# A hybrid attention and pooling layer: the first four blocks' order written out by hand, with scores between halves of projections

## The chip, the cores and the metric

The kernel runs on one core of one Trainium2 chip. Times are device microseconds of one execution. The program's engines are TensorE (PE, with its weight loads PEld), VectorE (DVE), ScalarE (ACT), GpSimd (POOL) and SyncE (SP), which issues all of the DMA transfers spoken of here.

## The reference

One layer of an encoder over 4096 tokens of width 1024: `x + RMSNorm_post(W_out [attn * silu(g_a) ; pool * silu(g_p)])`, where q, k, v, g_a, u_p and g_p come from one projection of the normed x.

```python
# q: 8 heads of 64; k, v: 2 heads; blocks of 128 queries see 3 blocks of keys
s = jnp.einsum('bnqkgd,bnskd->bnkgqs', qb, kw).astype(jnp.float32) * scale
s = jnp.where(valid, s + bias, NEG)               # |i - j| <= 128, T5 bias
m = jnp.maximum(jnp.max(s, axis=-1, keepdims=True), sk)   # learned sink
p = jnp.exp(s - m)
p = p / (jnp.sum(p, axis=-1, keepdims=True) + jnp.exp(sk - m))
o = jnp.einsum('bnkgqs,bnskd->bnqkgd', p, vw)
...
mean = (cg[:, hi] - cg[:, lo]) / (hi - lo)        # pooling windows 2, 4, 8, 16
y = (mean - u) @ pool_w[g] * pool_scale
```

## The kernel before

Every fp32 product is made of three fp16 products: each operand is kept as a high part and a rest, and PE multiplies high by high, high by rest and rest by high. So each result that PE needs again is read from its PSUM bank twice: ACT writes the high part and DVE (for Q, K and V, `split`, L1216 and L1217) or POOL (for the gated values, `low`, L1478) the rest. Until the second has been written, PE can neither use the result nor overwrite its bank.

The first stage, up to about 497 us, makes the projections g_p, u_p and g_a and leaves the pooling branch and the gates in DRAM (`yp_scr`, `ga_scr`). Its last part also makes K of unit 15. The second stage works on units of 256 tokens, from unit 15 down to 0. A unit u has the blocks 2u + 1 and 2u, of 128 queries each, and a block has two halves of four heads. Its steps on PE:

- `proj_k` and `proj_v` (L1361, L1365): K and V of the unit, 24 and 48 matmuls into one bank, kept by `keep_k` and `keep_v` (the tiles `k_all` and `vv`)
- `proj_q(u, half, bank)` (L1388): 48 matmuls, two pairs of heads of 24 each, into the bank `acc0` or `acc1` (tile `aq`), kept by `keep_q` (tile `q`)
- `scores(b, half)` (L1247, matmul L1272): 48 small matmuls into two banks of their own
- `values(b, bank)` (L1405, matmul L1422): probabilities by V, for both halves; one side goes to a bank of its own, the other to `acc0`, `acc1` or `acc2`
- `product` (L1564, matmul L1572): one of seven products of the gated values with pieces of W_out (`O11`, `O21`, `O22`, `OT1` to `OT4`, in the tiles `wo0` and so on, 1 MB each, loaded by `load_wo`, L1642), 12 matmuls of 512 columns. Seven products in place of eight come from sums of the halves (`sum1` to `sum4`, L1505 to L1516; the last on POOL).

Between scores and values lies the softmax of a half block: POOL copies the sink into the tile `p` (L1289), DVE makes logits and their maximum (L1295, four operations), ACT the exponentials (`exps`, L1306), DVE the denominators (L1313, L1316), ACT the scaled probabilities (`probs`, L1328), DVE their rests (`rests`, L1336), and SP issues a transposing DMA (`turn`, L1345, tile `pt`). The mixing of a unit goes on with `begin` (ACT copies one bank to the tile `mo0`, L1590), `gain11` (DVE, L1600), `add` (DVE, L1611), `square` (ACT, L1595), `gain` (POOL, L1606), `mean`, `residual` (DVE, L1633) and `store` (SP, L1639). The tiles `mo0` and `mo1` hold a block's result until its residual has been added.

The order of all of this is a plan: `due(t, fn, ...)` puts a step into a list with a time, and at the end (L1924) the list is sorted by these times and issued in that order, on every engine. The times are thus only an order; each engine works through its own queue and waits where an operand or a buffer is not ready. `pe(us, ...)` advances a clock `now[0]` for PE's steps, and `visit(b, half)` plans scores and softmax of a half block; `free` holds when DVE and ACT are through with the last one. Up to the second block from the end, one loop (L1743 to L1798) plans the steps of a block from these helpers; blocks 31 to 28 take branches of their own in it. The two last blocks are a table of numbers written by hand with `at_`, `soft` and `cast` (from L1802).

Of the kernel before, what the change touches and what calls it, by code (L numbers as in the profile page):

```python
# [17 lines left out]
P = 128  # L18
# [116 lines left out]
def hybrid_layer(ctx: ExitStack, tc, io, out):  # L135
# [74 lines left out]
    with ExitStack() as actx:  # L210
# [1032 lines left out]
    def due(t, fn, *args):  # L1243
        plan.append((t, len(plan), fn, args))
# [441 lines left out]
    def mix_p1(u):  # L1686
        due(pe(M, product, u, "11", O11, 0) - 1.0, begin, u)

    def mix_p4(u):
        pe(M, product, u, "22", OT4, 2)  # L1690

    def mix_p2(u):
        t = pe(M, product, u, "12", O21, 0, True)
        due(t, gain11, u)
        due(t + 0.1, square, u, 0, 0, 0)

    def mix_p6(u):
        due(pe(M, product, u, "s2", OT2, 1), add, u, (0, HI), (0, HI), 1)

    def mix_p7(u):  # L1700
        t = pe(M, product, u, "s3", OT3, 0)
        due(t - 2.0, add, u, (1, HI), (0, HI), 0)
        due(t - 1.9, add, u, (1, LO), (1, HI), 2)
        due(t + 1.4, square, u, 1, 0)
        due(t + 2.0, gain, u, 1, LO)

    def mix_p5(u):
        t = pe(M, product, u, "s1", OT1, 1)
        due(t, add, u, (1, HI), (1, HI), 1)
        due(t + 0.7, square, u, 1, 1)  # L1710
        due(t + 1.4, gain, u, 1, HI)
        finish(u, 1, t + 4.0)

    def mix_p3(u):
        t = pe(M, product, u, "s4", O22, 1, True)
        due(t, add, u, (0, HI), (0, HI), 1)
        due(t + 0.7, square, u, 0, 1)
        due(t + 1.4, gain, u, 0, HI)
        due(t + 4.0, mean, u, 0)
        due(t + 12.4, residual, u, 0, LO)  # L1720
        due(t + 13.1, residual, u, 0, HI)
        due(t + 13.8, store, u, 0, slice(0, D))

    def finish(u, i, t):

# [3 lines left out]

    u = NU - 1
    for o in (OT4, O11, O21, OT2):
        due(0.0, load_wo, o)
    due(0.1, load_gain)
    due(0.1, pool_in, u, 0)
    due(0.1, pool_in, u, 1)
    do_kv(u)

    due(now[0] + 1.0, lambda: nc.scalar.activation(dummy, mhalf, AF.Exp))  # L1740
    do_q(u, 0)
    now[0] += 1.0
    for b in reversed(range(2, NB)):  # L1743
        u = b // 2
        t0 = now[0]
        due(t0 + 10.0, load_ga, b)
        if b % 2 == 0 and 0 < b < NB - 2:
            due(t0 + 9.0, load_xr, u + 1, 1)
            due(t0 + 9.0, load_xr, u + 1, 0)
        visit(b, 0)  # L1750
        if b == NB - 1:
            do_q(u, 1, 2.8, 0)
            due(now[0] + 0.1, load_x, u - 2)
            now[0] += 2.5
            visit(b, 1)
            do_kv(u - 1, 2, 2.5)
            now[0] += 3.0
        elif b == NB - 3:
            due(free[1], load_wo, OT3)
            mix_p4(u + 1)  # L1760
            mix_p1(u + 1)
            attend(b + 1, 1)
            visit(b, 1)
            due(free[1], load_wo, OT1)
            due(free[1] + 8.0, load_wo, O22)
            do_kv(u - 1, 1)
            mix_p2(u + 1)
            mix_p6(u + 1)
        elif b % 2:
            mix_p3(u + 2)  # L1770
            do_kv(u - 1)
            attend(b + 1, 0)
            visit(b, 1)
            mix_p4(u + 1)
            mix_p1(u + 1)
            mix_p6(u + 1)
            mix_p2(u + 1)
        else:
            do_q(u - 1, 0, 2.0 * (b == NB - 2))
            if b < NB - 2:  # L1780
                attend(b + 1, 0)
            visit(b, 1)
            do_q(u - 1, 1, 2.0 * (b == NB - 2), int(b < NB - 2))
            due(now[0] + 2.1, load_x, u - 3)
            if b == NB - 2:
                attend(b + 1, 1)
            elif b > 2:
                mix_p7(u + 1)
# [11 lines left out]
    z = now[0]  # L1802
# [199 lines left out]
```

## Time and profile before

| | |
|---|---|
| median of 3 runs | 1193.59 us (1192.48 to 1194.16) |
| the profiled execution | 1192.04 us |
| its span in the trace | 1190.3 us |
| PE, DVE, ACT, POOL busy, share of the span | 97%, 79%, 59%, 25% |
| mean granted clock of PE | 0.997 |
| second stage's first four blocks | 497.3 to 583.5 us |
| the loop over the blocks behind them, and the end | 583.5 to 1092.3 us, and to 1190.3 us |

The profile's engines are as above; an engine's idle time is put down to what released it, so that `[2.88 <-ACT q L1216]` reads: idle for 2.88 us, until ACT's write of a tile `q` in line 1216 came. Tiles are shown there without their numbers. Busy time of PE counts pipelined matmuls whose ends are modelled. The granted clock is the share of full speed that the TensorE was given.

### The profile page before, as it was taken

What the parts mean: (1) busy time and instruction counts of PE and PEld (TensorE: products, weight loads), DVE (VectorE), ACT (ScalarE), POOL (GpSimd) and SP (SyncE); (2) the same over time, 40 slices, a digit from 0 to 9 for tenths busy, and PEclk for the clock granted to TensorE, in tenths of its full rate; (3) what the DMA queues carried; (4) which work ended last, traced back from release to release, by engine and by line L of the source; (5) the groups of instructions that cost most, each with busy time, mean ns of one, the idle gap of its engine ahead of it and who ended that gap; (6) DMA issues with size and microseconds to landing.
All of it is one profiled execution on the core that took longest, in us unless ns stands there. A gap on an engine that the chain in (4) does not pass through costs nothing. (4 is left out here: it accounts for less than half of the span.)

```text
span 1190.3 us, 33985 instructions
## 1 busy us (share of the span) xinstructions
PE 1154.4 (97%) x14304; PEld 884.8 (74%) x14304; DVE 941.9 (79%) x1879; ACT 703.8 (59%) x1459; POOL 303.4 (25%) x309
## 2 busy tenths in 40 slices
PE   5999999999999999998999999999999999999997
PEld 4998888888988888876667667576666667757643
DVE  6889996867888973567877878877887787787796
ACT  5865555545755541265666576666667667666662
POOL 0002111101101110203334434433533443343231
PEclk9999999999999999999999999999999999999999
DMA  9544587577657573397966876787886678586694
GB/s 318 208 124 151 169 277 246 171 239 259 221 169 249 156 212 117 117 242 174 253 181 147 188 189 128 200 196 142 192 193 177 145 191 192 135 190 164 156 245 124
DMA packets 292441, 224.65 MB, mean 189 GB/s; under 512 B 210704, under 2 KB 251920, under 8 KB 287680
## 3 DMA queue, kind: packets, MB, share of 16 engines
q1 hardware_dynamic: 292288, 222.48, 69.7%
q8 instruction: 112, 1.84, 0.6%
q14 instruction: 41, 0.34, 0.1%
HBM read 113.37 MB, written 60.33 MB: 146 GB/s over the span
## 5 line engine op out<-in xcount | busy, mean ns | idle before, releaser
L634 PEld LDWEIGHTS <-wq 128*128 128x128 f16 x4104 | 401.3, 98 | 53.1 <-issue 2.8
L634 PE MATMUL y<-xt,wq 128*128 128x256 f16 x1512 | 204.1, 273 | 0.9 <-ACT cc L742 0.9
L1336 DVE SCALAR_TENSOR_TENSOR pn<-p,rd,pn 128x384 f16<-128x384 f32 (+1 forms) x256 | 155.6, 654 | 31.8 <-ACT pn L1328 31.8
L1227 PE MATMUL aq<-xb,xb 128*128 128x256 f16 x1024 | 174.8, 274 | 1.7 <-DVE q L1217 1.6
L1306 ACT ACTIVATE p<-p,nm 128x385 f32<-128x385 f32 (+1 forms) x256 | 152.8, 598 | 33.3 <-POOL p L1289 22.4
L1572 PE MATMUL ms<-wo,ys 128*128 128x512 f16 x720 | 163.1, 379 | 1.7 <-ACT pn L1328 0.9
L1295 DVE CUSTOM_DVE_ANT_0 p<-s,nt,nsink 128x384 f32<-128x384 f32 (+1 forms) x256 | 155.9, 666 | 1.3 <-PE s L1272 1.1
L1328 ACT ACTIVATE pn<-p,rd 128x384 f16<-128x384 f32 (+1 forms) x256 | 136.4, 598 | 13.4 <-ACT p L1306 8.5
L1227 PEld LDWEIGHTS <-xb 128*128 128x128 f16 x1280 | 125.7, 98 | 23.3 <-issue 6.6
L1227 PE MATMUL aq<-xb,xt 128*128 128x256 f16 x512 | 140.3, 274 | 0.0
L1572 PEld LDWEIGHTS <-ys 128*128 128x128 f16 x720 | 69.0, 98 | 83.9 <-issue 3.3
L304 POOL TENSOR_TENSOR yt<-yt,sg 128x512 f32<-128x512 f32 (+2 forms) x32 | 48.0, 1501 | 311.3 <-DVE yt L307 302.3
L1572 PE MATMUL m<-wo,y 128*128 128x512 f16 x540 | 121.7, 379 | 2.8 <-ACT mo L1590 1.7
L1572 PEld LDWEIGHTS <-y 128*128 128x128 f16 x540 | 51.4, 98 | 68.3 <-issue 8.2
L1606 POOL TENSOR_TENSOR mo<-mo,gpost 128x512 f32<-128x512 f32 x39 | 63.6, 1630 | 86.8 <-ACT jkb L1595 85.7
L634 PE MATMUL plain<-xb,wq 128*128 128x256 f16 x576 | 68.8, 275 | 3.2 <-ACT xb L446 1.8
L1227 PEld LDWEIGHTS <-xt 128*128 128x128 f16 x640 | 62.9, 98 | 10.1 <-issue 1.5
L634 PE MATMUL y<-xb,wq 128*128 128x256 f16 x504 | 68.8, 273 | 0.0
L634 PE MATMUL v<-xb,wq 128*128 128x256 f16 x504 | 68.6, 273 | 0.2 <-DVE cc L304 0.2
L1272 PE MATMUL s<-k_all,q 64*32 64x288 f16 (+7 forms) x3648 | 62.9, 266 | 5.9 <-ACT q L1216 3.6
L634 PE MATMUL v<-xt,wq 128*128 128x256 f16 x504 | 68.6, 273 | 0.0
L634 PE MATMUL x<-xb,wq 128*128 128x256 f16 x504 | 68.3, 273 | 0.0
(211 smaller groups left out, 1917.1 us busy)
## 6 DMA issues: line engine op xcount, KB each, us to landing
nt<-in_xT SPq DMA_DIRECT2D x28, 512.0 KB, 5.2
x_scr<-xb SPq DMA_DIRECT2D x14, 1024.0 KB, 7.1
xb<-x_scr SPq DMA_DIRECT2D x14, 1024.0 KB, 7.6
xr<-in_x SPq DMA_DIRECT2D x28, 512.0 KB, 4.6
out<-xr SPq DMA_DIRECT2D x28, 512.0 KB, 2.8
xn<-in_x SPq DMA_DIRECT2D x27, 512.0 KB, 4.3
ga_scr<-cc SPq DMA_DIRECT2D x64, 128.0 KB, 2.2
raw<-in_w_out SPq DMA_DIRECT2D x16, 512.0 KB, 6.3
```

Source lines behind the costliest of these rows:

```text
L304: eng.tensor_tensor(out=out, in0=in0, in1=in1, op=op)
L634: nc.tensor.matmul(b[:, s], wq[:, slot[q, op], wv, s, k, :], x[:, xv, k, :], start=(first and k + s + wv + xv == 0), stop=(last and k == H ...
L1227: nc.tensor.matmul(acc, w[:, j, k, :], x[:, kh, v, kt, :], start=(n == 0), stop=(n == 3 * KT - 1),)
L1272: nc.tensor.matmul(s_ps[qs, gg, c0:c1], q_t[u, half][a, qi, jj, tl + 32 * hq : tl + 32 * hq + 32], k_all[a, ki, kc + c0 - s0 : kc + c1 - s ...
L1295: nc.vector.tensor_tensor_reduce(out=p_t[b, half][:, hh, :nk], in0=s_t[jj][:, gg, :nk], in1=bias[:, h, lo : lo + nk], scale=negc[:, h : h ...
L1306: nc.scalar.activation(p[:, hh, : nk + 1], p[:, hh, : nk + 1], AF.Exp, bias=nm_t[b, half][:, hh : hh + 1], scale=-1.0, accum_out=den_t[b, ...
L1328: nc.scalar.activation(prob_view(b, half)[:, 0, i], p_t[b, half][:, i, :nk], AF.Copy, scale=rd_t[b, half][:, i : i + 1],)
L1336: nc.vector.scalar_tensor_tensor(out=pn4[:, 1, i], in0=p_t[b, half][:, i, :nk], scalar=rd_t[b, half][:, i : i + 1], in1=pn4[:, 0, i], op0= ...
L1572: nc.tensor.matmul(z_t[u, tag], y[:, k, yi, :], wo[o][:, wi, k, :], start=(n == 0 and acc is None), stop=(n == 3 * HK - 1), skip_group_che ...
L1606: eng.tensor_tensor(out=mo, in0=mo, in1=gpost[:, cs], op=ALU.mult)
```

## The change

The blocks 31, 30, 29 and 28 leave the loop, and a table of numbers takes their place; the loop now begins at block 27. `proj_q1` plans half of a Q projection, one pair of heads. The diff, cut to its core:

```diff
+    def proj_q1(u, half, jj, bank):
+        if jj == 0:
+            kv_t[u, half] = gemm.tile([P, 2, UT], F32, name=f"aq{u}_{half}", tag=f"acc{bank}")
+        project_t(kv_t[u, half][:, jj], B_Q + 2 * half + jj, x_half(u))
...
     def open_unit(u):
-                pb.tile([P, D], F32, name=f"mo{u}_{i}", tag=f"mo{i}", bufs=1) for i in range(2)
+                pb.tile([P, D], F32, name=f"mo{u}_{i}", tag=f"mo{i}", bufs=2 - i) for i in range(2)
...
     def do_q(u, half, late=0.0, bank=1):
-        due(pe(5.3, proj_q, u, half, bank) - half + late, keep_q, u, half)
+        due(pe(5.3, proj_q, u, half, bank) - 1.0 + late, keep_q, u, half)
...
     def mix_p3(u):
-        t = pe(M, product, u, "s4", O22, 1, True)
-        due(t, add, u, (0, HI), (0, HI), 1)
+        bank = int(u < NU - 1)
+        t = pe(M, product, u, "s4", O22, bank, True)
+        due(t, add, u, (0, HI), (0, HI), bank)
...
-        due(t + 12.4, residual, u, 0, LO)
-        due(t + 13.1, residual, u, 0, HI)
-        due(t + 13.8, store, u, 0, slice(0, D))
+        due(t + 13.1, residual, u, 0, slice(0, D))
+        due(t + 14.5, store, u, 0, slice(0, D))
...
-    for o in (OT4, O11, O21, OT2):
-        due(0.0, load_wo, o)
...
-    due(now[0] + 1.0, lambda: nc.scalar.activation(dummy, mhalf, AF.Exp))
...
+        (5.4, proj_q, U, 0, 0),
+        (10.8, proj_q1, U, 1, 0, 1),
+        (13.5, scores, NB - 1, 0),
+        (14.3, proj_q1, U, 1, 1, 1),
+        (17.0, proj_k, U - 1, 2),
+        (19.7, scores, NB - 1, 1),
...
+    at_(0.0, lambda: nc.scalar.activation(dummy, mhalf, AF.Exp))
...
+    cast(26.0, 26.6, U, "22", a22, G)
+    cast(26.2, 27.0, U, "12", a12, G)
...
+    at_(58.1, square, U, 0, 0, 0)
+    at_(58.2, gain11, U)
...
+    at_(20.3, load_wo, O21)
+    at_(26.6, load_wo, OT2)
...
+    at_(67.1, load_wo, O22)
...
+    for b in reversed(range(2, NB - 4)):
...
-    at_(4.8, add, 2, (1, HI), (0, HI), 0)
+    at_(3.7, add, 2, (1, HI), (0, HI), 0)
...
-    at_(23.45, add, 1, (0, HI), (0, HI), 1)
+    at_(22.3, add, 1, (0, HI), (0, HI), 1)
```

The new order of PE's steps in the first four blocks is, with `Q15.0` for the Q projection of unit 15, half 0, and `a` and `b` for its halves: Q15.0, Q15.1a, scores 31.0, Q15.1b, K14, scores 31.1, V14, Q14.0a, scores 30.0, Q14.0b, Q14.1a, scores 30.1, Q14.1b, values 31, product 22, scores 29.0, K13, V13, scores 29.1, product 11, values 30, product 12, scores 28.0, Q13.0, product s2, values 29, scores 28.1, Q13.1, products s3 and s1, scores 27.0, product s4, K12. Before it was: Q15.0, scores 31.0, Q15.1, scores 31.1, K14, V14, scores 30.0, Q14.0, scores 30.1, Q14.1, values 31, scores 29.0, products 22 and 11, values 30, scores 29.1, K13, V13, products 12 and s2, scores 28.0, Q13.0, values 29, scores 28.1, Q13.1, products s3 and s1, scores 27.0, product s4, K12. On ACT, `dummy`, the exponential that makes ACT load its table, goes ahead of the casts of K of unit 15; before, it stood behind the casts of K and V and ahead of the first cast of Q. `mo0` gets a second buffer; since that pool grows by 4096 bytes a partition, `k_all` and the other tiles behind it lie 4160 bytes higher.

Where the scores of block 31, half 0, begin, PE's program before has them behind the last matmul of the projection whose result they read (`aq15_0` is that projection's bank, `q15_0` what its casts write; a number behind a name is that of its buffer):

```order
L1227 LDWEIGHTS xt0_67
L1227 MATMUL aq15_0_6047<-xb1_68,xt0_67 128x256
L1227 LDWEIGHTS xb0_66
L1227 MATMUL aq15_0_6047<-xb1_68,xb0_66 128x256
L1272 LDWEIGHTS q15_0_6100
L1272 MATMUL s0_5946<-k_all_5959,q15_0_6100 32x256
```

and the changed program at the same scores:

```order
L1227 LDWEIGHTS xt0_67
L1227 MATMUL aq15_1_6095<-xb1_68,xt0_67 128x256
L1227 LDWEIGHTS xb0_66
L1227 MATMUL aq15_1_6095<-xb1_68,xb0_66 128x256
L1272 LDWEIGHTS q15_0_6120
L1272 MATMUL s0_5946<-k_all_5959,q15_0_6120 32x256
```

The first pair of heads of the other half's projection, `aq15_1`, now lies between them.

On POOL, from the sink's copy into the tile of block 30's first half to the last cast of unit 15, before (`y22`, `y12`, `y11`, `ys1` to `ys4` are the operands of the products, `p` the tiles of the softmax, `yf1` the result of `sum4`):

```order
L1289 COPY p30_0_6484<-nsink_87 128x4
L1289 COPY p30_1_6610<-nsink_87 128x4
L1478 TENSOR_TENSOR y22_15_6676<-yf0_15_5993,y22_15_6676 128x4x128
L1478 TENSOR_TENSOR y12_15_6681<-yf1_15_5995,y12_15_6681 128x4x128
L1478 TENSOR_TENSOR y11_15_6743<-at31_6689,y11_15_6743 128x4x128
L1289 COPY p29_0_6765<-nsink_87 128x4
L1289 COPY p29_1_6965<-nsink_87 128x4
L1478 TENSOR_TENSOR ys2_15_6968<-at31_6689,ys2_15_6968 128x4x128
L1516 TENSOR_TENSOR yf1_15_5995<-yf1_15_5995,at31_6689 128x512
L1478 TENSOR_TENSOR ys3_15_7074<-at30_6874,ys3_15_7074 128x4x128
L1478 TENSOR_TENSOR ys1_15_7078<-s1_15_6927,ys1_15_7078 128x4x128
L1478 TENSOR_TENSOR ys4_15_7131<-yf1_15_5995,ys4_15_7131 128x4x128
```

and after:

```order
L1483 TENSOR_TENSOR y22_15_6405<-yf0_15_5990,y22_15_6405 128x4x128
L1483 TENSOR_TENSOR y12_15_6455<-yf1_15_5992,y12_15_6455 128x4x128
L1289 COPY p30_0_6490<-nsink_87 128x4
L1289 COPY p30_1_6614<-nsink_87 128x4
L1483 TENSOR_TENSOR y11_15_6756<-at31_6681,y11_15_6756 128x4x128
L1289 COPY p29_0_6791<-nsink_87 128x4
L1289 COPY p29_1_6933<-nsink_87 128x4
L1483 TENSOR_TENSOR ys2_15_7151<-at31_6681,ys2_15_7151 128x4x128
L1521 TENSOR_TENSOR yf1_15_5992<-yf1_15_5992,at31_6681 128x512
L1289 COPY p28_0_7169<-nsink_87 128x4
L1483 TENSOR_TENSOR ys3_15_7283<-at30_7033,ys3_15_7283 128x4x128
L1483 TENSOR_TENSOR ys1_15_7337<-s1_15_7036,ys1_15_7337 128x4x128
```

The copies into `p30_0` and `p30_1` moved behind the two casts `y22` and `y12`, and the copy into `p28_0`, which before stood behind `ys4`, moved up to the place right behind `sum4`.

On SP, from the load of `wo4` (OT1) to the second transpose of block 28, before (`wo3` is O22, `yf0_14` and `yf1_14` are the pooling operands of unit 14, `xr` the rows of x for the residual, `gb` the gates, `xb1` the x of a unit to come):

```order
L1642 DMA wo4_5954<-w_scr_98 128x4096
L1501 DMA yf0_14_7076<-yp_scr_95 128x512
L1501 DMA yf1_14_7191<-yp_scr_95 128x512
L1642 DMA wo3_5953<-w_scr_98 128x4096
L1345 DMA_TRANSPOSE pt28_0_7338<-pn28_0_7200 128x24x128
L1619 DMA xr30_7340<-in_x 128x1024
L1619 DMA xr31_7342<-in_x 128x1024
L1403 DMA gb28_7402<-ga_scr_96 128x512
L1213 DMA xb1_68<-x_scr_94 128x4096
L1345 DMA_TRANSPOSE pt28_1_7441<-pn28_1_7416 128x24x128
```

and after:

```order
L1647 DMA wo4_5954<-w_scr_98 128x4096
L1506 DMA yf0_14_7153<-yp_scr_95 128x512
L1408 DMA gb28_7157<-ga_scr_96 128x512
L1624 DMA xr30_7160<-in_x 128x1024
L1624 DMA xr31_7162<-in_x 128x1024
L1506 DMA yf1_14_7179<-yp_scr_95 128x512
L1345 DMA_TRANSPOSE pt28_0_7339<-pn28_0_7199 128x24x128
L1647 DMA wo3_5953<-w_scr_98 128x4096
L1213 DMA xb1_68<-x_scr_94 128x4096
L1345 DMA_TRANSPOSE pt28_1_7441<-pn28_1_7416 128x24x128
```

The load of `wo3` now stands behind the first transpose of block 28, and the loads of `gb28` and of the rows of x ahead of it. Four of W_out's pieces stood at the head of SP's queue before (`OT4`, `O11`, `O21`, `OT2`); now `O21` stands behind the transpose of block 31's first half and `OT2` behind that of its second.

More of the change, by code (lines that the diff above doesn't have):

```diff
@@ L1826, in ending @@
             at_(tr + 1.3 + 0.7 * n, store, u, i, cs)
+    z = 0.0
+    U = NU - 1
+    for t, fn, *args in (
+        (0.0, proj_k, U, 2),
+        (2.6, proj_v, U),
+        (5.4, proj_q, U, 0, 0),
[4 more added lines that the diff above has]
+        (19.7, scores, NB - 1, 1),
+        (20.6, proj_v, U - 1),
+        (23.4, proj_q1, U - 1, 0, 0, 0),
+        (26.1, scores, NB - 2, 0),
+        (27.2, proj_q1, U - 1, 0, 1, 0),
+        (29.9, proj_q1, U - 1, 1, 0, 1),
+        (32.6, scores, NB - 2, 1),
+        (33.7, proj_q1, U - 1, 1, 1, 1),
+        (36.4, values, NB - 1, 0),
+        (38.4, product, U, "22", OT4, 2),
+        (41.0, scores, NB - 3, 0),
+        (42.0, proj_k, U - 2, 1),
+        (44.7, proj_v, U - 2),
+        (47.5, scores, NB - 3, 1),
+        (48.4, product, U, "11", O11, 0),
+        (51.1, values, NB - 2, 1),
+        (53.1, product, U, "12", O21, 0, True),
+        (55.7, scores, NB - 4, 0),
+        (56.7, proj_q, U - 2, 0, 1),
+        (62.1, product, U, "s2", OT2, 0),
+        (64.7, values, NB - 3, 1),
+        (66.7, scores, NB - 4, 1),
+        (67.6, proj_q, U - 2, 1, 0),
+        (73.0, product, U, "s3", OT3, 1),
+        (75.6, product, U, "s1", OT1, 0),
+    ):
+        at_(t, fn, *args)
@@ new lines, in hybrid_layer @@
+    at_(10.8, keep_q, U, 0)
+    at_(11.0, keep_v, U)
+    at_(17.05, keep_q, U, 1)
+    at_(23.5, keep_k, U - 1)
+    at_(25.9, keep_v, U - 1)
+    cast(26.0, 26.6, U, "22", a22, G)
+    cast(26.2, 27.0, U, "12", a12, G)
+    at_(33.9, keep_q, U - 1, 0)
+    at_(38.35, gate, NB - 1)
+    at_(38.37, keep_q, U - 1, 1)
+    cast(41.0, 41.6, U, "11", a11, G)
+    at_(48.2, keep_k, U - 2)
+    at_(48.6, keep_v, U - 2)
+    at_(51.3, begin, U)
+    at_(53.1, gate, NB - 2)
+    at_(53.2, sum1, U)
+    at_(54.1, sum3, U)
@@ new lines, in hybrid_layer @@
+    at_(57.1, sum2, U)
+    cast(58.0, 58.7, U, "s2", a11, G)
+    at_(58.1, square, U, 0, 0, 0)
+    at_(58.2, gain11, U)
+    at_(59.0, sum4, U)
+    at_(63.3, keep_q, U - 2, 0)
+    at_(64.75, add, U, (0, HI), (0, HI), 0)
+    cast(66.2, 66.8, U, "s3", a21, G)
+    at_(66.75, gate, NB - 3)
+    cast(66.8, 67.4, U, "s1", a_s1, G)
+    cast(67.4, 68.0, U, "s4", a12, G)
+    cast(67.5, 68.6, U - 1, "11", a11, G)
+    at_(72.0, keep_q, U - 2, 1)
+    at_(73.6, add, U, (1, HI), (0, HI), 1)
+    at_(73.7, add, U, (1, LO), (1, HI), 2)
@@ new lines, in hybrid_layer @@
+    at_(77.0, square, U, 1, 0)
+    at_(77.6, gain, U, 1, LO)
+    at_(78.2, add, U, (1, HI), (1, HI), 0)
+    at_(78.9, square, U, 1, 1)
+    at_(79.6, gain, U, 1, HI)
+    finish(U, 1, 82.2)
+    at_(0.0, load_wo, OT4)
+    at_(0.1, pool_in, U, 0)
+    at_(0.1, pool_in, U, 1)
+    at_(0.1, load_gain)
+    at_(0.2, load_wo, O11)
+    at_(17.1, load_x, U - 2)
+    at_(20.2, load_ga, NB - 1)
+    at_(20.3, load_wo, O21)
+    at_(26.6, load_wo, OT2)
+    at_(34.6, load_ga, NB - 2)
+    at_(36.5, load_x, U - 3)
@@ L1829, in hybrid_layer @@
+    z = now[0]
     at_(0.0, scores, 1, 0)
```

114 lines of the change are left out of this document (50 added, 64 removed).

## The prediction

> **What bounds the kernel now.** I read the page first.
>
> ```profile
> span 1190.3 us, 33985 instructions
> ...
> PE 1154.4 (97%) x14304; PEld 884.8 (74%) x14304; DVE 941.9 (79%) x1879; ACT 703.8 (59%) x1459; POOL 303.4 (25%) x309
> ...
> L1306 ACT ACTIVATE p<-p,nm 128x385 f32<-128x385 f32 (+1 forms) x256 | 152.8, 598 | 33.3 <-POOL p L1289 22.4
> ```
>
> TensorE works for 97% of the span, and the change keeps its matmuls: a gain can come only from its idle time, or from matmuls at a lowered clock. Where that lies is shown by windows over the four first blocks, the loop behind them and the end (columns: length, busy time and instructions of PE, PEld, DVE, ACT and POOL, granted clock, DMA share, GB/s).
>
> ```profile
> 497.30:583.50 86.20, 77.64 (x1144) 57.09 (x1142) 54.96 (x146) 51.19 (x133) 15.13 (x21) 0.98 0.86 228
> 583.50:1092.30 508.80, 504.73 (x7633) 344.51 (x7632) 411.46 (x936) 328.33 (x817) 198.22 (x204) 1.00 0.76 175
> 1092.30:1190.30 98.00, 90.02 (x1105) 52.04 (x1103) 78.17 (x170) 54.06 (x139) 29.05 (x31) 0.98 0.66 171
> 507.00:510.50 3.50, 3.50 (x26) 2.56 (x19) 2.08 (x10) 2.56 (x10) 0.00 (x0) 0.53 1.01 426
> 546.00:549.50 3.50, 3.39 (x108) 2.84 (x108) 2.50 (x6) 0.67 (x2) 0.00 (x0) 1.00 0.02 5
> ```
>
> The first window is what the list replaces: 86.20 - 77.64 = 8.56 us idle in 86. PE's waits (us in total, times, longest), first in 497 to 583, then two rows of 583 to 1125:
>
> ```profile
> PE s L1272 <- ACT q L1216: 3.6, 2, 2.9
> PE o L1422 <- DMA pt<-pn: 1.4, 1, 1.4
> PE ms L1572 <- ACT pn L1328: 0.9, 1, 0.9
> PE s L1272 <- DVE q L1217: 0.8, 2, 0.4
> PE m L1572 <- POOL y L1478: 0.7, 1, 0.7
> PE aq L1227 <- DVE q L1217: 0.6, 1, 0.6
> PE s L1272 <- ACT k_all L1216: 0.5, 1, 0.5
> ...
> PE m L1572 <- ACT mo L1590: 1.7, 9, 0.2
> PE aq L1227 <- DVE q L1217: 1.1, 6, 0.2
> ```
>
> Here a wait can only be a cast that was queued too late. The worst, at the scores of block 31, on PE and then on ACT (start, length, in brackets the idle time and its releaser):
>
> ```profile
> 505.57 0.30 PE L1272 MATMUL s<-k_all,q 64*32 64x256 f16 x8 [2.88 <-ACT q L1216]
> ...
> 506.30 0.74 PE L1272 MATMUL s<-k_all,q 64*32 64x256 f16 x40 [0.42 <-DVE q L1217]
> ...
> 502.26 0.38 ACT L1216 ACTIVATE k_all<-kv 128x256 f16<-128x256 f32 x1 [4.77 <-DMA ga_scr<-cc]
> ...
> 503.54 1.28 ACT L1740 ACT_TABLE_LOAD   x1
> ...
> 504.94 0.58 ACT L1216 ACTIVATE q<-aq 128x512 f16<-128x512 f32 x1
> ```
>
> PE stands 2.88 and 0.42 us for casts behind a late K cast and a table load of 1.28 us; then the clock is 0.53 for 3.5 us (the window 507.00 to 510.50), which costs 3.50 x 0.47 = 1.65 us.
>
> **The change part by part: first stretch.** The list holds the same steps, with half a Q projection or a K projection between any Q and its scores. I add to each recorded gap the refill that it costs beyond itself. In the loop:
>
> ```profile
> 719.64 5.35 PE L1572 MATMUL m<-wo,y 128*128 128x512 f16 x24
> 724.83 2.75 PE L1572 MATMUL ms<-wo,ys 128*128 128x512 f16 x12
> 727.78 2.75 PE L1572 MATMUL m<-wo,y 128*128 128x512 f16 x12 [0.20 <-ACT mo L1590]
> 730.46 0.93 PE L1272 MATMUL s<-k_all,q 64*32 64x288 f16 x48
> 731.32 0.28 PE L1227 MATMUL aq<-xb,xb 128*128 128x256 f16 x1
> ...
> 736.67 0.25 PE L1422 MATMUL o<-pt,vv 128*64 128x128 f16 x2
> ...
> 738.59 0.93 PE L1272 MATMUL s<-k_all,q 64*32 64x288 f16 x48
> 739.70 0.27 PE L1227 MATMUL aq<-xb,xb 128*128 128x256 f16 x1 [0.18 <-DVE q L1217]
> ```
>
> Start to start, a product takes 5.19 / 2 = 2.60 us, scores 0.86, a Q projection 5.35, values 1.92. The product with the 0.20-us gap delays by 2.95 - 2.60 = 0.35, so a gap costs 0.16 more than it shows. Old cost of the stretch: 8.5 (the waits, nine of them) + 9 x 0.16 + 1.65 (clock) = 11.6 us.
>
> All of that goes if the list works: K's cast has no stores to wait for (its tile lies elsewhere, since one tag grew), the table is loaded ahead of it, and each cast has at least 2.6 us of matmuls to hide behind. What is late next? I walked the new order from 497.3 with these durations: both scores of block 31 find their casts done; five waits are left.
>
> 1. POOL now has the casts y22 and y12 ahead of the copy into p30_0, which exps30_0 needs.
>
> ```profile
> 535.41 2.69 POOL L1478 TENSOR_TENSOR y<-yf,y 128x512 f16<-128x512 f32 x2 [13.68 <-ACT y L1474]
> ...
> 553.00 1.28 POOL L1516 TENSOR_TENSOR yf<-yf,at 128x512 f32<-128x512 f32 x1
> ...
> 564.12 0.62 ACT L1306 ACTIVATE p<-p,nm 128x385 f32<-128x385 f32 x1 [2.60 <-POOL p L1289]
> ...
> 545.93 0.25 PE L1422 MATMUL o<-pt,vv 128*64 128x128 f16 x2 [1.39 <-DMA pt<-pn]
> ```
>
> They take 2.69 us, so block 30's softmax starts some 2 us late and q14_1's casts end near 533.6, where PE would begin K of unit 13 (same bank) at 533.1: 0.55 us (0 to 1.0).
>
> 2. The values of block 30 would begin at 542.4; unit 13's V casts stand on ACT behind exps29_0 and probs29_0 (8 operations of about 0.6, the row of L1306: 4.8 us), near 543.5: 1.1 (0 to 2.1; the transpose lands no earlier than 5.1 us behind its issue, below).
>
> 3. begin stands behind one of block 29's exponentials: 0.4 (0 to 0.8).
>
> 4. The values of block 29 use the bank of Q of unit 13. Its cast follows exps28_0, whose copy follows ys2 and the 1.28-us sum on POOL. Before, exps28_0 waited 2.60 us for that copy, and no projection stood behind. The sum ended at 554.3, some 7 us after block 30's values, which went on at 545.93; now they end near 545.5, and DVE has more rests between: 555.3. Four exponentials, the cast on ACT and its second half on DVE, about 0.6 each, and the hand-overs make 4.0: 559.3 against 557.15 on PE: 2.2 (0 to 3.2).
>
> 5. The load of O22. On SP (with wo's landing and then pt's, from issue, least, median, most):
>
> ```profile
> 564.57 0.58 SPq L1642 DMA_DIRECT2D wo<-w_scr  x1
> 571.10 4.79 SPq L1345 DMA_TRANSPOSE pt<-pn  x1
> ...
> DMA to landing us min/median/max: 5.3/8.6/9.3
> ...
> DMA to landing us min/median/max: 5.1/5.9/10.5
> ```
>
> O22's load was issued at 564.57, ahead of the transpose of block 28; now it stands behind it, and that behind yf1, which waits for POOL's last cast of unit 15 (564.8 in the walk). A transpose holds SP 3.8 to 4.8 us: issue near 569.1, landing at 574.4 to 578.4. PE wants it at 573.5. I take 575.5, nearer the least because few loads are in flight there: 2.0 us (0.9 to 4.9).
>
> [...]
>
> New waits: 0.55 + 1.1 + 0.4 + 2.2 + 2.0 = 6.25, with five refills 7.05. The stretch gains 11.6 - 7.05 = 4.55 us. Were all five at their high ends (12.0 + 0.8), it would lose 1.2; at their low ends (0.9 and one refill), gain 10.5.
>
> **The loop.** begin writes mo0, and the rows of its line name the previous unit's residual as releaser, 13 times of 13:
>
> ```profile
>   DVE xr L1633: 19.4, 13
> ```
>
> A second buffer removes that wait; begin then waits only for its product. PE's nine waits for it go: 9 x 0.35 = 3.15 us. Cover: exps end before the product that needs begin. The Q cast one us sooner stands ahead of the four probs; the wait at 739.70 delays by 738.59 to 739.70 = 1.11 against 0.86: 6 x 0.25 = 1.5. Each may come out at 0 if ACT is late for another reason, and the probs, which go one cast (0.58) later, could hand the Q term on to the values: together 4.65 (-1.5 to 4.65).
>
> **At nothing:** the residual in one operation instead of two, later (two buffers cover it); the two adds in the tail sooner (DVE is busy 78.17 of 98 us there; -0.7 to +1.4); gb, xr and x loads in new places (wanted many us later); the O21 and OT2 loads behind transposes, issued by about 525 in the walk, wanted at 545 and 554, and landing within 9.3; were that cover gone, PE would stop for as long as they are late.
>
> **Sum.** 4.55 + 4.65 = 9.2 us. The profiled execution took 1192.04 (span 1190.3), so 1182.8. The median of the runs is 1193.59, 1.55 above it: 1184.4.
>
> **Rivals.**
>
> *A. The five new waits hardly come*, because my walk has ACT or POOL late by more than they are, and O22 lands in 5.3. For it: each is under 2.3 us. Stretch 10.5, loop 4.65: 1193.59 - 15.15 = 1178.4. Chance 0.14.
>
> *B. The loop's waits stay*, handed to the next cast in ACT's queue: only 4.55, so 1189.0. For it: DVE and ACT are within some tenths of PE at those places. Against: the releaser is always the same, and is removed. 0.15.
>
> *C. Half clock again.* The rows show it after 2.88 + 0.42 us of waits, not after 1.39 (the window 546.00 to 549.50, granted 1.00). Waits of 2.2 and 2.0 lie between. Each drop costs 1.65: one gives 1186.1, two 1187.7. 0.15.
>
> [...]
>
> *D. Slower: O22 far too late.* Nothing fills PE at that product. Landing at 575.5 is assumed; the gain of 9.2 and the 2.4 us that count as slower are used up with a drop of the clock (1.65) when it lands 9.95 us later, near 585.5, which is 16.4 us behind its issue. The worst here is 9.3. Price at 20 us behind its issue (589.1): 13.6 + 1.65, so 1199.7. For it: the load shares the queues with x and xr loads and transposes. 0.05.
>
> *E. No change:* several of these waits at their high ends and the loop's staying: 1193.6. 0.05.
>
> **How the numbers follow.** The forecast has 0.46, with a range of its own of 1180 to 1188 (O22 at its ends, -1.1 to +2.9, with some of the others' spread). Low 1178.5 leaves out about half of A; high 1189.5 holds B and C and leaves out D and E: 0.17 outside. About 0.2% (2.4 us) can be told from no change in this kernel. Faster: forecast, A, B and C, 0.90; same 0.05; slower 0.05.
>
> **What would show it.** Right: PE's waits in the first stretch near 6 us in place of 8.5, no clock of 0.53 near 507, K of unit 12 starting some 5 us sooner; in the loop no waits for mo and Q. Step 4 shows as a wait of the values for the cast of q, step 5 as one for the wo load. Wrong: a clock below 1 after 557 or 574, mo waits with a new releaser, or a wait for wo above 5 us.

## The result and the profile after

The changed kernel takes 1180.88 us (median of 4 runs, 1180.44 to 1183.24) against 1193.37 for the kernel before (4 runs, 1192.48 to 1194.16): 12.5 us less, a ratio of 0.990 with a 95% interval of 0.9882 to 0.9917. The forecast was 1184.4 in a range of 1178.5 to 1189.5. The profiled execution took 1180.83 us, with a span of 1178.7. On the page:

```profile
span 1178.7 us, 33947 instructions
...
PE 1149.8 (98%) x14304; PEld 883.1 (75%) x14304; DVE 932.8 (79%) x1866; ACT 702.8 (60%) x1459; POOL 308.6 (26%) x309
```

The same three stretches, cut where the same steps begin (the Q projection of unit 15, K of unit 12, K of unit 0), and the window in which the clock had been 0.53:

```profile
498.40:579.10 80.70, 75.40 (x1143) 55.95 (x1141) 55.35 (x146) 51.17 (x134) 15.24 (x21) 1.00 0.94 248
579.10:1081.70 502.60, 502.03 (x7633) 343.66 (x7632) 403.05 (x924) 327.43 (x815) 203.00 (x204) 1.00 0.75 176
1081.70:1178.70 97.00, 89.60 (x1105) 51.90 (x1103) 76.97 (x169) 54.00 (x140) 29.46 (x31) 0.98 0.70 173
507.00:510.50 3.50, 3.50 (x47) 3.05 (x32) 2.22 (x10) 2.64 (x10) 0.00 (x0) 1.00 1.04 355
```

The first stretch is 5.4 us shorter, the loop 6.2, the tail 1.0. Everything before the first stretch is 1.1 us longer in this execution (the Q projection starts at 498.38 instead of 497.29; the difference arises in the first 30 us, ahead of all that was changed, and the other traces of the changed order have it at 496.9 to 497.9), so times below are compared with the walk 1.1 us later. PE's waits in the first stretch, then in the loop with its beginning:

```profile
PE p L1427 <- DVE vv L1217: 1.2, 1, 1.2
PE p L1427 <- DVE q L1217: 1.1, 1, 1.1
PE m L1577 <- ACT mo L1595: 0.5, 1, 0.5
PE kv L1227 <- DVE q L1217: 0.3, 1, 0.3
...
PE ms L1577 <- DMA wo<-w_scr: 2.2, 1, 2.2
PE s L1272 <- issue: 0.6, 1, 0.6
```

These are the five waits of the walk, at the five places; the view, which leaves out waits under 0.15 us, lists no others in the first stretch. All nine old rows are gone. On PE the first scores now begin without a gap, and the last of the five waits stands ahead of the product with O22:

```profile
506.33 0.85 PE L1272 MATMUL s<-k_all,q 64*32 64x256 f16 x48
...
560.09 0.25 PE L1427 MATMUL p<-pt,vv 128*64 128x128 f16 x2 [1.15 <-DVE q L1217]
...
576.55 2.75 PE L1577 MATMUL ms<-wo,ys 128*128 128x512 f16 x12 [2.19 <-DMA wo<-w_scr]
```

On ACT, K's cast follows the table load at once, where it had been idle for 4.77 us:

```profile
498.60 1.28 ACT L1809 ACT_TABLE_LOAD   x1
...
500.00 0.36 ACT L1216 ACTIVATE k_all<-kv 128x256 f16<-128x256 f32 x1
503.82 0.60 ACT L1216 ACTIVATE q<-aq 128x512 f16<-128x512 f32 x1 [3.45 <-PE aq L1227]
```

And in the loop, at the place that the prediction read (unit 11), the s2 product takes 2.59 from start to start in place of 2.95, and the scores 0.86 in place of 1.11:

```profile
718.93 2.75 PE L1577 MATMUL ms<-wo,ys 128*128 128x512 f16 x12
721.52 2.75 PE L1577 MATMUL m<-wo,y 128*128 128x512 f16 x12
...
732.33 0.93 PE L1272 MATMUL s<-k_all,q 64*32 64x288 f16 x48
733.19 0.28 PE L1227 MATMUL aq<-xb,xb 128*128 128x256 f16 x1
```

### The profile page after: what moved, and what is told of

Read it like the earlier page. It is cut to its first block, busy times and chain, and to the rows that moved or that the text cites. A ratio compares the mean times of both kernels' runs of the same rounds, so it can differ in the third digit from the quotient of the medians.

```text
span 1178.7 us, 33947 instructions
## 1 busy us (share of the span) xinstructions
PE 1149.8 (98%) x14304; PEld 883.1 (75%) x14304; DVE 932.8 (79%) x1866; ACT 702.8 (60%) x1459; POOL 308.6 (26%) x309
## 4 chain that ended last, share of the span: by engine, by line
PE 48%; DVE 2%; DMA 1%; ACT 1%; issue 0%; DVEq 0%; POOLq 0%; SPq 0%; ACTq 0%
PE aq L1227 12%; PE ms L1577 12%; PE m L1577 9%; PE s L1272 4%; PE kv L1373 3%; PE kv L1227 3%; PE o L1427 3%; PE p L1427 2%; PE z L1549 1%; DVE pn L1336 1%; DVE p L1295 0%; DMA wo<-w_scr 0%; DMA pt<-pn 0%; PE s L1549 0%; ACT pn L1328 0%
## 5 line engine op out<-in xcount | busy, mean ns | idle before, releaser
L1427 PEld LDWEIGHTS <-vv 128*64 128x64 f16 (+1 forms) x2256 | 55.1, 109 | 12.4 <-issue 6.8
```

Of the source, the lines that this page charges most:

```text
L1427: nc.tensor.matmul(o_t[b][side][a, half], v_t[ku][ks, vi, kt, a], pt[b, half][ks, pi, g, :, kb - kbs[0], (LOW, TOP)[side]], start=start, s ...
```

## The experiments

My theory was the prediction's: waits on PE add up, each removed wait is worth its gap and a refill, and a new one costs the same. Against it stood that removed waits are handed on, and, of the first stretch, a question that the prediction had left open: it counted the new place of `k_all` in memory, a side effect of the second buffer, together with the new order of the steps. Which of them made the gain?

All runs in one table. The lengths of the three stretches, in us, are taken from the starts of the same three steps in the one trace of each kernel; "before" is the median of the runs of the kernel before beside it.

| run | median, us | before, us | ratio, 95% interval | first | loop | tail |
|---|---|---|---|---|---|---|
| kernel before | | | | 86.18 | 508.83 | 98.00 |
| changed kernel | 1180.88 | 1193.37 | 0.9882 to 0.9917 | 80.76 | 502.60 | 96.96 |
| changed, once more | 1180.93 | 1192.51 | 0.9891 to 0.9918 | 80.46 | 502.77 | 96.96 |
| second buffer alone | 1181.84 | 1192.39 | 0.9895 to 0.9922 | 82.49 | 503.00 | 97.32 |
| longer tile alone | 1188.76 | 1192.51 | 0.9956 to 0.9978 | 82.80 | 508.73 | 98.11 |
| Q cast sooner alone | 1190.99 | 1192.39 | 0.9979 to 0.9996 | 84.64 | 507.00 | 97.93 |
| changed, one buffer | 1187.58 | 1192.39 | 0.9947 to 0.9972 | 80.36 | 509.28 | 98.01 |
| changed, scores back | 1184.54 | 1192.39 | 0.9913 to 0.9940 | 85.18 | 502.99 | 96.93 |
| changed, table back | 1179.80 | 1192.03 | 0.9889 to 0.9918 | 80.20 | 502.79 | 96.91 |
| changed, tail back | 1180.90 | 1192.03 | 0.9892 to 0.9922 | 80.70 | 502.57 | 97.31 |
| changed, O22 sooner | 1178.09 | 1192.03 | 0.9872 to 0.9901 | 78.60 | 502.75 | 96.91 |
| changed, O22 later | 1184.68 | 1192.51 | 0.9927 to 0.9952 | 85.00 | 503.07 | 96.98 |
| changed, five waits | 1176.74 | 1192.03 | 0.9856 to 0.9889 | 77.34 | 502.91 | 96.97 |
| five waits, and two more | 1177.65 | 1192.51 | 0.9864 to 0.9891 | 78.69 | 503.05 | 96.95 |

### The second buffer alone

```diff
 # kernel before
-    pb.tile([P, D], F32, name=f"mo{u}_{i}", tag=f"mo{i}", bufs=1) for i in range(2)
+    pb.tile([P, D], F32, name=f"mo{u}_{i}", tag=f"mo{i}", bufs=2 - i) for i in range(2)
```

> The kernel before with nothing but the second buffer for mo0. Theory (two effects of one edit): in the loop (K of unit 12 to K of unit 0) begin no longer waits for the residual, and the twelve s2 products go from 2.95 to 2.60 us, about 3.4 us less; and since the tag grows, k_all lies elsewhere, K's first cast no longer waits 4.77 us for stores, the scores of block 31 wait near 0.7 + 0.4 us as the second half's do, and the half clock at 507 is gone: 2.2 + 1.65 = 3.9 us less in the first stretch. Together 1193.4 - 7.3 = 1186.1. Rival 1 (the first stretch gains by the interleaved order alone, the layout does nothing): the first stretch stays at 86.2 us, 1190.0. Rival 2 (begin's wait is handed to the next cast): the loop stays at 508.8 us, 1193.4 or 1189.5 with the layout's part.

It brings 10.6 us, more than I expected; the whole change brought 12.5, and 11.6 in its second measurement. The loop falls by 5.8 instead of 3.4: PE's recorded waits for begin and those for the Q cast are both gone, though the Q cast stands where it stood. The first stretch falls by 3.7. Its windows:

```profile
497.30:579.80 82.50, 75.97 (x1144) 56.23 (x1142) 54.94 (x146) 51.28 (x133) 15.12 (x21) 1.00 0.88 237
579.80:1082.80 503.00, 502.19 (x7634) 343.70 (x7633) 412.49 (x936) 328.15 (x817) 198.91 (x204) 1.00 0.75 177
```

### The longer tile alone

One buffer, but with room for two, which moves `k_all` and the tiles behind it and changes nothing else:

```diff
 # kernel before
-    pb.tile([P, D], F32, name=f"mo{u}_{i}", tag=f"mo{i}", bufs=1) for i in range(2)
+    pb.tile([P, D * (2 - i)], F32, name=f"mo{u}_{i}", tag=f"mo{i}", bufs=1)[:, :D]
+    for i in range(2)
```

> The kernel before with one buffer for mo0 as before, but twice as long, the second half never used: every instruction and its order stay, only the tiles behind it, k_all among them, lie 4160 bytes higher. Theory (the place of k_all is what shortened the first stretch of the second-buffer run): first stretch from 86.2 to 82.5 us, no clock of 0.53 at 507, loop unchanged at 508.8: 1192.2 - 3.7 = 1188.5. Rival (the second buffer itself did it): 86.2 us and 1192.2.

1188.76 and 82.80: as the theory had it. The loop and the tail do not move. K's cast no longer waits:

```profile
497.61 0.38 ACT L1216 ACTIVATE k_all<-kv 128x256 f16<-128x256 f32 x1
```

The first stretch, the loop and the window in which the clock had been 0.53; then the first two waits on PE, which had been 2.88 and 0.42:

```profile
497.40:580.20 82.80, 76.13 (x1144) 56.11 (x1142) 54.97 (x146) 51.30 (x133) 15.05 (x21) 1.00 0.88 239
580.20:1088.90 508.70, 504.39 (x7634) 344.43 (x7633) 411.58 (x936) 328.28 (x817) 198.32 (x204) 1.00 0.75 175
507.00:510.50 3.50, 3.26 (x30) 2.68 (x28) 2.03 (x6) 2.30 (x7) 0.19 (x1) 1.00 1.00 421
```

```profile
503.45 0.30 PE L1272 MATMUL s<-k_all,q 64*32 64x256 f16 x8 [0.69 <-ACT q L1216]
504.18 0.74 PE L1272 MATMUL s<-k_all,q 64*32 64x256 f16 x40 [0.42 <-DVE q L1217]
```

So 3.4 us of the first stretch (3.75 in the medians) come from an address: at its old place the cast into `k_all` waited for the end of a store that reads the first stage's tile `cc` (the 4.77 us of the prediction's row); at its new place it does not.

### The Q cast sooner alone

```diff
 # kernel before
-        due(pe(5.3, proj_q, u, half, bank) - half + late, keep_q, u, half)
+        due(pe(5.3, proj_q, u, half, bank) - 1.0 + late, keep_q, u, half)
```

> The kernel before with nothing but the Q casts one us sooner. Theory: the waits of the second Q projection for the first one's cast go, 1.5 us by the prediction's count of six, about 2.0 by the steps' lengths in the two traces: 1191.4. Rival (the time is handed on to the values, whose probabilities are now later): 1193.4.

The loop falls by 1.8, near the 2.0. The first stretch of this trace is 1.5 us shorter too, though its waits for the Q cast, 2.68 and 0.42, are nearly as long as before: the clock stayed full behind them in this execution, the fastest of its 11 (its mean clock is 0.999, that of the other ten 0.996 to 0.998). The part on the rivals below comes back to this.

To see why the two edits do not add up in the loop, I summed its steps from start to start by kind: the twelve s2 products, behind which begin is waited for, the 48 scores, behind which Q is waited for, and the 24 values.

| loop, us | s2 products | scores | values |
|---|---|---|---|
| before | 34.47 | 46.72 | 46.99 |
| Q cast sooner alone | 34.75 | 44.81 | 46.63 |
| second buffer alone | 31.08 | 44.88 | 46.24 |
| changed kernel | 31.09 | 44.62 | 46.08 |

Each edit alone cures the waits for Q. Before, six of the 48 scores took 1.11 us and one 0.94 where the same ones take 0.86 with either edit: 1.6 us. The rest of that column is a single pause, put down to `issue`, of 1.0 us before, 0.8 with either edit and 0.6 in the changed kernel, which neither edit explains. The buffer alone also cures the waits for begin (-3.4: eight s2 products of 2.94 or 2.95 and three of 2.75 to 2.78, all 2.59 now). The values' difference comes from three places: 0.42 us at one of them, gone only with the buffer, and 0.5 at the first two, which the longer tile alone removes as well.

### One buffer again

```diff
 # changed kernel
-    pb.tile([P, D], F32, name=f"mo{u}_{i}", tag=f"mo{i}", bufs=2 - i) for i in range(2)
+    pb.tile([P, D], F32, name=f"mo{u}_{i}", tag=f"mo{i}", bufs=1) for i in range(2)
```

> The changed kernel with one buffer for mo0 again, which also puts k_all back to its old place. Theory: the loop's waits for begin come back, 3.4 us, at least as long as before since the residual is now one later operation; the first stretch stays near 80.7 us, since the scores of block 31 are 2.6 us of matmuls further from the K cast: 1184.3, up to 1186 if the later residual lengthens the waits. Rival (the layout carries the first stretch in the new order too): K's cast waits for the stores until 502 or later and the first scores wait with a half clock: 1187 to 1188.

The first stretch stays (80.36) though `k_all` is back at its old place: K's cast waits for the store again, but the scores are 2.6 us of matmuls further off and do not wait for it:

```profile
502.81 0.38 ACT L1216 ACTIVATE k_all<-kv 128x256 f16<-128x256 f32 x1 [3.25 <-DMA ga_scr<-cc]
```

The new order and the new place are two cures for the same wait. The loop costs more than I expected, 6.7 us and not 3.4 to 5: PE now waits for begin 11 times and up to 0.5 us, where it was 0.2 at most in the rows of before. Begin's releaser is the residual, 12 times of 12; that it comes later because it is now one later operation was not tried by itself.

```profile
PE m L1577 <- ACT mo L1595: 4.3, 11, 0.5
```

### Scores back behind their projection

```diff
 # changed kernel
-        (10.8, proj_q1, U, 1, 0, 1),
-        (13.5, scores, NB - 1, 0),
+        (10.9, proj_q1, U, 1, 0, 1),
+        (10.85, scores, NB - 1, 0),
...
-        (17.0, proj_k, U - 1, 2),
-        (19.7, scores, NB - 1, 1),
+        (17.1, proj_k, U - 1, 2),
+        (17.06, scores, NB - 1, 1),
```

> The changed kernel with both scores of block 31 directly behind the Q projection that they read, as before the change; all else as changed. Theory: each waits for its casts as the second half did before, 0.69 + 0.42 and two refills, 1.4 us; two of them 2.8, less what the later waits of the stretch give back (0.3 to 1.2): 1182.5 to 1183.7. Rival 1 (K's place and the table load did it all, the interleaving nothing): 1180.9. Rival 2 (the old 2.9-us wait and half clock return): 1186.

Both waits came as expected, 0.69 + 0.42 each. But the stretch is 4.4 longer and not 2.8. The rest is at the product with O22: its wait is 2.58, and the product takes 4.17 in place of 2.75. The product, and two windows of 3.41 us each, the second behind the wait:

```profile
578.51 4.17 PE L1577 MATMUL ms<-wo,ys 128*128 128x512 f16 x12 [2.58 <-ACT p L1306]
```

```profile
576.27:579.68 3.41, 1.17 (x6) 0.60 (x7) 1.96 (x8) 2.76 (x10) 1.27 (x1) 1.00 1.01 348
579.68:583.09 3.41, 3.41 (x11) 1.37 (x10) 0.37 (x1) 0.00 (x0) 0.00 (x0) 0.50 1.14 286
```

The clock was halved behind that wait: 2.8 + 0.4 + 1.4 = 4.6, against 4.4 measured. The row names an exponential as releaser, but the load of O22, issued at 573.12, landed 5.3 us later, 0.1 us before the product went on: the load ended this wait, as in the changed kernel.

### Table load back

```diff
 # changed kernel
-    at_(0.0, lambda: nc.scalar.activation(dummy, mhalf, AF.Exp))
+    at_(10.75, lambda: nc.scalar.activation(dummy, mhalf, AF.Exp))
```

> The changed kernel with the exponential that loads ACT's table put back to its place ahead of the first Q cast, behind K's cast. Theory: ACT is idle for 3.45 us there, so the 1.28-us load hides: no change, 1180.9. Rival (the load waits for the Q projection's end, or starts late): up to 1.3 us more in the Q cast, hidden by 2.6 us of matmuls all the same, or 1182.2 if not.

No change: the load runs at 497.95, and ACT is idle for 3.29 us before the Q cast. With the other parts in place, the load's new place is worth nothing.

```profile
497.95 1.28 ACT L1809 ACT_TABLE_LOAD   x1
...
502.74 0.60 ACT L1216 ACTIVATE q<-aq 128x512 f16<-128x512 f32 x1 [3.29 <-PE aq L1227]
```

### The tail's adds back

```diff
 # changed kernel
-    at_(3.7, add, 2, (1, HI), (0, HI), 0)
+    at_(4.8, add, 2, (1, HI), (0, HI), 0)
...
-    at_(22.3, add, 1, (0, HI), (0, HI), 1)
+    at_(23.45, add, 1, (0, HI), (0, HI), 1)
```

> The changed kernel with the two adds of the tail at their old places. The prediction put them at nothing (-0.7 to +1.4); in the two traces the stretch from K of unit 0 to the end is 98.00 before and 97.00 after. Theory: the adds are that 1.0 us: 1181.9. Rival (the adds are nothing, and the 1.0 us is spread or chance): 1180.9.

The tail is 0.35 us longer, 97.31 against 96.96, which the medians can't tell. The other 0.7 of the tail's gain is there with the second buffer alone (97.32); the last wait for begin lies there.

### O22 sooner, and later

```diff
 # changed kernel; sooner, and in another run later
-    at_(67.1, load_wo, O22)
+    at_(59.0, load_wo, O22)
...
-    at_(67.1, load_wo, O22)
+    at_(73.2, load_wo, O22)
```

> The changed kernel with the load of O22 issued ahead of the load of yf1, so some 10 us sooner. Theory (PE's waits add up): the wait of 2.19 us for the load and a refill go: 2.3 us less, 1178.6. Rival (the wait is handed on to a later load or transpose in the same queue): 1180.9.

> The changed kernel with the load of O22 moved later still, behind the load of x for unit 11 in the queue. Theory (rivals C and D of the prediction: the product stands still until it lands, and a wait that is long enough brings the half clock): the load is issued 0.7 us later and shares the queues with 1 MB of x, landing 2 to 5 us later; the wait is 4.2 to 7.2 us in place of 2.19, and the clock falls as it did after 2.58: 1180.9 + 2.0 to 5.0 + 1.65 = 1184.5 to 1187.5. Rival (no half clock, the transfer hardly later): 1181.6 to 1183.

Sooner: the wait is gone, the first stretch 2.16 us shorter than that of the changed kernel, and nothing else is late. Later: the wait grows to 4.13, and the clock falls. The product, and the window from it:

```profile
578.07 4.44 PE L1577 MATMUL ms<-wo,ys 128*128 128x512 f16 x12 [4.13 <-DMA wo<-w_scr]
```

```profile
578.00:581.50 3.50, 3.43 (x10) 1.37 (x11) 0.00 (x0) 0.00 (x0) 0.00 (x0) 0.59 0.72 165
```

4.13 - 2.19 = 1.9 and the product's 4.44 - 2.75 = 1.7 make 3.6; with a pause of 0.5 put down to `issue` and its refill that is about the 4.2 by which this trace's first stretch is longer. The medians differ by 3.75. The load was issued no later than in the changed kernel, 72.9 us behind the start of Q of unit 15 in both, but PE went on 7.8 us behind the issue in place of 5.3. This is rival D's mechanism, at a small dose.

### The five waits, and two more

```diff
 # changed kernel
-    at_(38.35, gate, NB - 1)
+    at_(38.4, gate, NB - 1)
...
-    at_(48.2, keep_k, U - 2)
-    at_(48.6, keep_v, U - 2)
-    at_(51.3, begin, U)
+    at_(45.84, keep_k, U - 2)
+    at_(45.86, keep_v, U - 2)
+    at_(50.05, begin, U)
...
-    at_(59.0, sum4, U)
-    at_(63.3, keep_q, U - 2, 0)
-    at_(67.1, load_wo, O22)
+    at_(59.5, sum4, U)
+    at_(61.28, keep_q, U - 2, 0)
+    at_(59.0, load_wo, O22)
```

> The changed kernel with the causes of all five waits of its first stretch taken away: O22's load sooner, q14_1's cast ahead of the gate on DVE, unit 13's K and V casts ahead of block 29's probabilities, begin ahead of its exponentials, the sink's copy ahead of the last sum on POOL and unit 13's Q cast between the exponentials of block 28. Theory (they add up): 0.27 + 1.24 + 0.46 + 1.15 + 2.19 = 5.31 and five refills 0.8: 6.1 us less, 1174.8. Rival (what is moved back is waited for in its turn): 3 us less or under.

4.2 us less than the changed kernel in the medians, 3.4 in the first stretch: neither the 6.1 of the theory nor the rival's 3 or less. The five waits are gone, but some of the time is handed on. What is late next:

```profile
PE o L1427 <- DMA pt<-pn: 0.9, 1, 0.9
PE p L1427 <- DVE q L1217: 0.3, 1, 0.3
PE aq L1227 <- issue: 0.2, 1, 0.2
```

These are 1.4 us, and short pauses that the list leaves out add to them. Behind the V cast stood the transpose of block 30's second half, which now ends the wait of the same values. For that I moved the load beside it, and more:

```diff
 # five waits
-    at_(36.5, load_x, U - 3)
+    at_(41.85, load_x, U - 3)
...
-    at_(38.4, gate, NB - 1)
+    at_(41.3, gate, NB - 1)
...
-    cast(41.0, 41.6, U, "11", a11, G)
+    cast(41.4, 41.6, U, "11", a11, G)
...
-    at_(61.28, keep_q, U - 2, 0)
+    at_(60.5, keep_q, U - 2, 0)
```

> The kernel of the five waits with what was late behind them moved too: the load of x for unit 12 behind the second transpose of block 30, block 31's gate behind block 30's rests, unit 13's Q cast one exponential sooner. Theory (the 0.95 us for the transpose and the 0.28 for the cast go): 1.5 us less than the five-waits kernel's 1176.7, so 1175.2. Rival (the transposes are slow by themselves there, or the load is missed): 1176.7 or more.

A miss: the first stretch is 1.35 us longer than with the five waits, and the medians, 1177.65 and 1176.74, can't tell the two apart. The waits for the transpose and the Q cast are gone, but DVE has become the one that is late:

```profile
PE aq L1227 <- DVE mo L1616: 1.4, 1, 1.4
PE ms L1577 <- DVE mo L1605: 1.0, 1, 1.0
PE m L1577 <- ACT mo L1595: 0.9, 1, 0.9
PE ms L1577 <- DVE mo L1616: 0.3, 1, 0.3
```

Which of the moves did this was not tried. The kernel with the five waits, 1176.74, is the fastest one run.

### The changed kernel once more

> The changed kernel once more, to stand beside the others on one chip. Both theories: 1180.9, within 1 us.

1180.93 against 1180.88: the time holds. Its wait for O22 is 1.5 us, and its first stretch 0.3 us shorter.

## Why the prediction came out as it did

- **The old cost of the first stretch, 11.6 us.** It holds. Without it the stretch would be 86.18 - 11.6 = 74.6; the changed kernel needs 80.76, that is 6.2 more, and its five recorded waits with five refills make 5.31 + 0.8 = 6.1. So the refill of 0.16 per gap, read from the loop, serves here too. The stretch gained 5.4 where 4.55 was forecast, because the new waits were 0.9 us shorter.
- **The five new waits, 6.25 forecast, 5.31 measured.** Forecast and measured: 0.55 and 0.27; 1.1 and 1.24; 0.4 and 0.46; 2.2 and 1.15; 2.0 and 2.19. Step 1 came out at half its size; step 4 was the one far off. The last sum on POOL ended where the walk had it, as the rows show (556.2 against 555.3 + 1.1), and PE went on at 560.09, against 559.3 + 1.1 = 560.4. But PE stopped only at 560.09 - 1.15 = 558.94, 0.7 later than 557.15 + 1.1. It reached these values only at 558.70, 0.45 later than in the walk, and ran 0.24 us of them before it stopped: the row names the tile `p`, the side that shares the bank, and the first matmuls of the values go into the other.

```profile
554.89 1.27 POOL L1521 TENSOR_TENSOR yf<-yf,at 128x512 f32<-128x512 f32 x1
556.11 0.19 POOL L1289 COPY p<-nsink 128x4 f32<-128x4 f32 x1
```

- **O22.** Its load was issued at 571.26, that is 570.2 in the walk's time against the 569.1 forecast, and landed 5.2 us later, where 575.5 - 569.1 = 6.4 had been taken. One error was 1.1 us late and the other 1.2 soon: that the wait came out at 2.19 for 2.0 is in part luck. PE went on 5.3 us behind the issue.

```profile
571.26 0.58 SPq L1647 DMA_DIRECT2D wo<-w_scr  x1
```

- **The loop, 4.65 forecast, 6.2 measured.** The terms for begin (3.15 against 3.4) and for Q (1.5 against 1.6) were right. Begin's was right by two slips that nearly cancel: one of its nine waits lies behind the loop, in the tail, and three short ones (0.16 to 0.19 us by the steps) are missing from the view, which leaves out what is under 0.15 us. What had been put at nothing is the rest: 0.9 from the values, and 0.46 from the one pause put down to `issue`, whose length differed from run to run, so that part is chance. And the split was wrong: I gave the Q waits to the sooner cast, but the buffer alone removes them too. Unit 11 shows the way by which the late begin reached the Q cast. ACT, in the kernel before:

```profile
727.14 0.59 ACT L1590 COPY mo<-m 128x512 f32<-128x512 f32 x1 [1.50 <-DVE xr L1633]
...
731.71 0.60 ACT L1595 ACTIVATE jkb<-m 128x512 bf16<-128x512 f32 x1 [0.53 <-DVE mo L1600]
...
734.31 0.62 ACT L1306 ACTIVATE p<-p,nm 128x385 f32<-128x385 f32 x1 [1.41 <-POOL p L1289]
```

Begin waits 1.50 us for the residual, so the probs behind it on ACT are late, then their rests and gain11 on DVE; for gain11 ACT's square waits 0.53 us. Behind the square stands the last cast of the unit, whose rest POOL writes ahead of its copies of the sink, and for these the exponentials ahead of the Q cast wait. With the buffer alone the same square waits for nothing, and DVE starts Q's rest 0.05 us ahead of the scores that PE runs before it needs that bank, where it had been 0.36 us behind their start:

```profile
726.09 0.60 ACT L1595 ACTIVATE jkb<-m 128x512 bf16<-128x512 f32 x1
```

- **The tail, nothing forecast, 1.0 measured:** 0.7 with the buffer, half of it begin's ninth wait, and 0.35 with the adds, inside the stated bounds of the latter. Taken together, the forecast was 3.5 us too high, and its misses, 0.9 in the stretch, 1.55 in the loop and 1.0 in the tail, all lie on one side.
- **What brings the gain.** The prediction's two terms, half for the first stretch and half for the loop, do not simply add up, because the parts cure the same waits. Put into the kernel before, one buffer more brings 10.6 us, 3.4 to 3.7 of them by moving `k_all`. On top of it, all else brings 1 to 2 us in the medians and 2.5 in the traces of the two kernels (82.49 to 80.76, 503.00 to 502.60 and 97.32 to 96.96): with the buffer alone the first stretch still holds 82.49 - 74.6 = 7.9 us of waits and refills, and the order puts 6.2 in their place. Taken the other way round, the changed kernel without the buffer is 4.8 us faster than the kernel before (1187.58), with 5.8 less in the first stretch, and the buffer brings 6.7 on top. With the rest in place the table load brings nothing.
- **Rivals.** A did not happen: the new waits are there. Nor did B: nothing is handed on in the loop. C did not happen in the profiled execution: the windows behind the waits of 1.15 and 2.19 (the first two rows) show full clock. It lies close by: 2.58 and 4.13 brought it. The one run of 1183.24 had a mean clock of 0.997 against 0.999 for the other three; that fits one such drop, but it was not profiled. D was right in its mechanism and far from its deciding point.

```profile
560.00:563.50 3.50, 3.41 (x125) 2.90 (x125) 3.50 (x6) 3.02 (x6) 1.44 (x2) 1.00 1.01 400
576.50:580.00 3.50, 3.45 (x20) 1.98 (x21) 0.82 (x4) 0.97 (x4) 0.00 (x0) 1.00 1.03 301
```

Why one wait lowers the clock and another does not is not a matter of its length alone, nor, in the windows here, of PE's busy time. The low stretch of the kernel before, 507.20 to 510.61, with the 3.41 us ahead of it:

```profile
503.79:507.20 3.41, 1.21 (x51) 0.78 (x51) 1.29 (x3) 1.72 (x3) 0.00 (x0) 1.00 0.99 408
507.20:510.61 3.41, 3.41 (x19) 2.43 (x17) 1.93 (x11) 2.67 (x10) 0.00 (x0) 0.50 1.02 430
```

The changed kernel, 3.41 us up to the end of its wait of 2.19 and as much behind it:

```profile
573.14:576.55 3.41, 1.23 (x50) 0.63 (x49) 3.29 (x9) 2.22 (x7) 2.76 (x3) 1.00 0.97 368
576.55:579.96 3.41, 3.41 (x20) 1.91 (x21) 0.73 (x4) 0.92 (x4) 0.00 (x0) 1.00 1.03 299
```

PE was busy for 1.21 us in the one window and for 1.23 in the other, and the clock fell to 0.50 behind the first alone; ahead of the low stretch of "scores back" it was 1.17. Windows at the waits of "tail back" (its wait for O22 was 2.17 us) and of "Q cast sooner alone" (two that share its waits of 2.68 and 0.42 us), both executions with a mean clock of 0.999, show PE busy for 1.50, and for 1.62 and 2.10 us, at a clock of 1.00:

```profile
571.36:574.77 3.41, 1.50 (x51) 0.70 (x49) 3.29 (x10) 2.21 (x9) 2.64 (x3) 1.00 0.94 353
...
500.41:503.82 3.41, 1.62 (x15) 1.20 (x13) 0.85 (x2) 1.92 (x3) 0.00 (x0) 1.00 0.87 280
503.82:507.23 3.41, 2.10 (x59) 1.58 (x60) 2.00 (x6) 1.49 (x6) 0.00 (x0) 1.00 1.02 428
```

These are few cases, and what decides between them was not shown.

## What to carry to other kernels

Before crediting an order of steps, look what a buffer added beside it does by itself, to waits and to addresses: a tile that moves can drop a wait for a store that has nothing to do with it, here one of 4.77 us. Run each part alone and also leave it out: two parts that cure the same wait do not add up. Count waits from the lengths of the steps, start to start, step by step over all repetitions: a list drops the short ones, and a sum takes in single pauses that have nothing to do with the change. When a wait is removed in a tight pipeline, walk the new order to the next late operand: here that walk found all five, each within 1.1 us.

## What the hardware showed

The granted clock fell to 0.50 for 3.41 us behind a wait of 2.58 us on PE ("scores back"; the product took 4.17 us in place of 2.75). Behind waits of 2.19 and 1.15 us it stayed full, and in one execution behind 2.68 and 0.42 us too ("Q cast sooner alone"). What told these apart was not shown: PE was busy for 1.21 us in the 3.41 us ahead of the low clock of the kernel before, and for 1.23 us in the 3.41 us up to the end of the wait of 2.19. A gap on PE cost about 0.16 us beyond its recorded length (a product took 2.95 us from start to start in place of 2.60 with a recorded gap of 0.20). The load of O22, 1 MB, landed 5.2 us (changed kernel) and 5.3 us ("scores back") after its issue; the loads of W_out's pieces, all of that size, landed after 5.3 to 9.3 us in the kernel before and after 5.1 to 9.9 us in the changed one.
